# Attention scores of a two-layer encoder: three fp32r passes over high and low parts, both heads of a pair per query tile

## The chip, the cores and the metric

One core of a Trainium2 chip runs the whole program. The metric is the device time of one execution in microseconds (us). The kernel before takes 1906.68 us, the median of three runs from 1904.6 to 1908.85 us.

## What is computed

Two layers of a bidirectional encoder over 768 tokens of 1024 features: one request of 512 tokens and one of 256, with one set of weights, all in fp32. A layer has a mixer (attention with 8 heads of 64 beside a convolution over 512 channels) and a gated feed-forward part. Cut to what matters here:

```
h = rms_norm(x, norm1_g[l]) * (1 + s1) + sh1
q, k, v, cv, cg = split(h @ w_in)                      # 512 columns each
q, k = rms_norm(q per head) * q_g, rms_norm(k per head) * k_g
for (window, dilation) in ((128, 1), (512, 4), (2048, 16)):
    s = q @ k.T * ATT_SCALE + bias[distance];  masked softmax;  o = p @ v
att = the three outputs, weighted by their softmax denominators
u = silu(layer_norm(depthwise_conv(cv * sigmoid(cg), 31 taps)))
x = x + g1 * (concat([att, u]) @ w_out)
x = x + g2 * conv_ffn(rms_norm(x, norm2_g[l]) * (1 + s2) + sh2)
```

The kernel folds the three patterns into one softmax per head, with the logarithm of each distance's number of patterns added to the bias.

## The kernel before

Activations lie with features on partitions and tokens along the free dimension, in two groups: 512 tokens (g = 0) and 256 (g = 1). A projection is exact to about fp32 by three fp32r passes (`three`, lines 346 to 348): weight and activation are each split into a high part (a copy to fp32r on ACT) and a low part (the rest, a subtraction on DVE). Weights come in units of eight 128x128 blocks: `load_ahead` issues the load into a raw buffer, `consume` makes the parts `wh` (line 324, ACT) and `wl` (line 325, DVE), `release` counts a unit as used.

The order of the instructions on every engine is the order in which the program emits them. It is set by a clock in microseconds of TensorE work: `tick(dt)` advances it, `after(dt, fn)` puts a piece of work on it for later, and two background streams are dealt out by it, the attention (`side`, one step each `gap`) and the 31 taps of the convolution (`conv_bg`, by a rate). `wait(key)` emits what is due, in order and with no projection between, until the key is done.

The mixer runs in this order: gate and value columns of the convolution (`c`, `cv`, `cg`), then `v`, `q`, `k` of the first four heads; with `attention()` as background `q`, `k`, `v` of the other four; then the output projection in three parts, `pa` (attention heads 0 to 3), `pb` (heads 4 to 7) and `pc` (convolution, which also starts the next norm). A pair of heads is one 128-partition tile of `qT` and `kT`, head s on partitions 64 s to 64 s + 63.

Attention goes in steps, one per pair, group, half of 256 queries, head s and query tile qi (128 queries). `start` (line 718) emits one fp32 matmul of 64 rows, queries by all keys of the group, into a bank of PSUM. Then, each some microseconds of the clock later: `soft` (DVE adds the bias and takes the minimum, line 735; ACT takes the exponential and its sum, line 737), `normal` (reciprocal on DVE, scaling on ACT, line 746), `turn` (PE transposes `tp`, line 759; ACT evacuates to `PT`, line 760) and, when both heads have both query tiles, `values_` (`o`, line 770, the two heads on the column halves of the array; then `cah`, `cal`). At most LIVE = 5 steps are in flight. The bias of a head lies in a table `G`, loaded by `bias_table`, in three buffers.

The convolution's taps (line 554) run on DVE. After the last one, `mean` (`lm`), `centre` (`lb`, four subtractions, squares, sums), `variance` (`lv`, a power on GpSimd), `scale_shift` (`lrb`, multiply, Silu, high and low parts `cch`, `ccl`) follow for each group, and `pc` needs them.

Of the kernel before, what the change touches and what calls it, by code (L numbers as in the profile page):

```python
# [12 lines left out]
F32 = mybir.dt.float32  # L13
# [5 lines left out]
P = 128  # L19
# [18 lines left out]
RAW = 5  # L38
ACT = 28
# [5 lines left out]
GAPS = (0.9, 0.9, 0.6)  # L45
# [7 lines left out]
NORM_ACT = True  # L53


@with_exitstack
def encoder(ctx: ExitStack, tc: tile.TileContext, xT, cT, rel_bias, onehot, nlog, wada, wadaT, wada_g2, bada,
# [34 lines left out]
    # ---- emission order: a clock in microseconds of TensorE work, work due later on it, and two background streams  # L92
# [57 lines left out]
    # ---- constants  # L150
# [30 lines left out]
    # ---- the weight stream: units of 8 [P, 128] blocks, in the order of their use  # L181
# [45 lines left out]
    state = {"item": 0, "live": 0, "n": 0, "fed": 0.0, "hold": True}  # L227
# [20 lines left out]
    def ada_columns(l, kind, j, ps):  # L248
        """kind 0, 1: scale and shift of feature tile j for the half-layer; kind 2: the first gate of tiles 2j, 2j + 1."""
# [56 lines left out]
    def consume():  # L306
# [3 lines left out]
        load_ahead(i + RAW)  # L310
        r = loaded[i]
        state["fed"] = clock[0]
        if it[0] == "a":
            ada(*it[1:], r)
            return
        if it[0] == "d":
            ada_dots(*it[1:], r)
            return
# [4 lines left out]
        lo = whl.tile([P, 8 * P], F32R, tag="lo", name=f"wl{n}")  # L323
# [9 lines left out]
    def unit():  # L333
        """The next unit of the stream as two lists of blocks (hi, lo)."""
        while not ready:
            consume()
        return ready.pop(0)

    def release(n=1):
        state["live"] -= n  # L340

# [12 lines left out]
    def product(units, xs, name, keys=None):  # L354
        """Several units side by side over the contraction: [unit][group] -> psum, features on partitions."""
# [13 lines left out]
    # ---- RMSNorm with its modulation  # L369
# [14 lines left out]
    def square_sums(l, h, g, hs):  # L384
        """Returns add(j), to be called when x[j] of the group is final; after the last one the normalised tiles follow."""
# [58 lines left out]
    def part(l, gate, xs, name):  # L444
        """A part of a projection back to the residual: contraction over xs, units of 8 // len(xs) output tiles."""
# [10 lines left out]
    def last_part(l, gate, xs, name, nxt, need=None):  # L456
        """The same with one group after the other, so that the next norm runs beside it."""
# [20 lines left out]
    # ---- constants of the layers and the bias by distance  # L478
# [43 lines left out]
    # ---- mixer  # L522

    def mixer(l, K, hs, nxt):
# [112 lines left out]
        def tokens(hh, name, evacuate):  # L637
            """Columns of a half of the heads, tokens on partitions, in three pairs of token tiles."""
# [25 lines left out]
        def qk(hh, t):  # L664
# [5 lines left out]
            def evacuate(pr, ps):  # L670
# [17 lines left out]
                def turn(qn):  # L688
# [7 lines left out]
                    for i in range(2):  # L696
                        nc.scalar.activation(dst[2 * hh + i][:, pr * 256:(pr + 1) * 256], pt[:, i * 256:(i + 1) * 256],
                                             AF.Copy, scale=gain)
# [7 lines left out]
        def attention():  # L706
            steps = [(hp, g, qh, s, qi) for hp in range(4) for g, (o, w) in enumerate(GROUPS) for qh in range(w // 256)
                     for s in range(2) for qi in range(2)]
            live = [0]
            pts = {}  # L710
            for n in range(3):
                bias_table(l, n)
            base = len(tables) - 3
            last = {}
            for n, (hp, g, qh, s, qi) in enumerate(steps):
                last[2 * hp + s] = n

            def start(n):
                hp, g, qh, s, qi = steps[n]
# [11 lines left out]
                def soft():  # L731
# [6 lines left out]
                    if last[2 * hp + s] == n and 2 * hp + s + 3 < NH:  # L738
# [314 lines left out]
```

## Time and profile before

| | |
|---|---|
| median of three runs | 1906.68 us |
| span of the profiled execution | 1912.8 us |
| PE (matmul) busy | 1855.5 us, 97% |
| weight loads | 1559.1 us, 82% |
| DVE busy | 1208.8 us, 63% |
| ACT busy | 642.9 us, 34% |
| GpSimd (POOL) busy | 205.3 us, 11% |
| mean granted TensorE clock | 0.988 |
| DMA | 164.75 MB, 86 GB/s |

The profiled execution has no time of its own beside its span; the span is 6.1 us above the median of the runs. Busy times are shares of the span, and PE's contains overlapping of neighbouring matmuls, so what a piece costs on PE is read from the starts of its neighbours. The mixer of layer 0 ends at 413.7 us, where its feed-forward part begins (`u`). A clock of 1.00 is 2.4 GHz, 0.50 is 1.2 GHz.

### The profile page before, as it was taken

Reading aid. Unit: us, or ns where it says so; the run is one execution under the profiler, and the core shown is the slowest. Engines: PE = TensorE matmul, PEld = TensorE weight load, DVE = VectorE, ACT = ScalarE, POOL = GpSimd, SP = SyncE. Lnnn points to the kernel's source line nnn. Section 1 sums busy time; section 2 is a strip of 40 time slices with the busy share of each in tenths; the row PEclk is TensorE's granted clock in tenths of the full one; section 3 lists DMA queues with packets and bytes.
Section 4 is the critical chain, followed back from the end, with each engine's and each line's share of the span. In section 5 each row is a group of like instructions: output and inputs, shape, how many; then the busy total and the mean of one; then the engine's idle time right before and its main releaser. Section 6 shows DMA issues by size and latency. Waiting matters only on the chain.

```text
span 1912.8 us, 27144 instructions
## 1 busy us (share of the span) xinstructions
PE 1855.5 (97%) x11164; PEld 1559.1 (82%) x11164; DVE 1208.8 (63%) x1964; ACT 642.9 (34%) x1130; POOL 205.3 (11%) x159
## 2 busy tenths in 40 slices
PE   6999999999999999999989999999899999999999
PEld 4788676778888888888878976767788888888888
DVE  6779666776766767665578886667744343434334
ACT  3222666443313121213232256564431222222220
POOL 1002110022101000101030120000410000000010
PEclk9999999999999999999999999999999999999999
DMA  9334210113334444443111111111112122221111
GB/s 336 125 128 167 64 53 32 40 44 120 118 122 123 142 133 133 130 134 99 56 56 56 56 63 42 42 43 45 48 63 84 49 67 67 66 67 56 56 56 66
DMA packets 54267, 164.75 MB, mean 86 GB/s; under 512 B 6176, under 2 KB 15648, under 8 KB 54144
## 3 DMA queue, kind: packets, MB, share of 16 engines
q1 hardware_dynamic: 54144, 163.03, 26.9%
q8 instruction: 87, 1.43, 0.3%
q14 instruction: 36, 0.29, 0.0%
HBM read 159.83 MB, written 3.18 MB: 85 GB/s over the span
## 4 chain that ended last, share of the span: by engine, by line
PE 84%; DVE 10%; ACT 3%; issue 2%; POOL 1%; DMA 0%; SPq 0%; ACTq 0%; DVEq 0%; POOLq 0%
PE g L346 6%; PE a L346 6%; PE g L347 6%; PE a L347 6%; PE g L348 6%; PE a L348 6%; PE pd L346 5%; PE pd L347 5%; PE pd L348 5%; PE s L725 4%; DVE acc L554 2%; PE tp L759 2%; DVE wl L325 2%; PE o L770 2%; PE v L346 1%
## 5 line engine op out<-in xcount | busy, mean ns | idle before, releaser
L325 DVE TENSOR_TENSOR wl<-raw,wh 128x1024 fp32r<-128x1024 f32 x186 | 264.8, 1433 | 132.4 <-ACT wh L324 132.4
L324 ACT ACTIVATE wh<-raw 128x1024 fp32r<-128x1024 f32 x188 | 191.8, 1049 | 208.7 <-PE pd L348 208.7
L554 DVE SCALAR_TENSOR_TENSOR acc<-up,cw_sb,acc 128x783 f32<-128x783 f32 x240 | 246.6, 1028 | 3.9
L862 DVE SCALAR_TENSOR_TENSOR gc<-g,fw_sb,gc 128x511 f32<-128x511 f32 x84 | 51.4, 612 | 228.7 <-ACT gc L861 228.7
L346 PE MATMUL pd<-hh,wl 128*128 128x512 f32 (+1 forms) x576 | 193.8, 336 | 0.0
L347 PE MATMUL pd<-hl,wh 128*128 128x512 f32 (+1 forms) x576 | 193.5, 336 | 0.0
L348 PE MATMUL pd<-hh,wh 128*128 128x512 f32 (+1 forms) x576 | 192.8, 335 | 0.0
L867 POOL TENSOR_TENSOR hl<-gc,hh 128x768 fp32r<-128x768 f32 x44 | 81.8, 1859 | 900.9 <-ACT hh L866 886.0
L861 ACT ACTIVATE gc<-g,fw_sb 128x512 f32<-128x512 f32 x84 | 48.1, 573 | 382.6 <-PE g L348 382.6
L441 DVE SCALAR_TENSOR_TENSOR x<-pd,mod,x 128x512 f32<-128x512 f32 (+1 forms) x160 | 92.4, 611 | 77.8 <-PE pd L348 77.7
L292 DVE CUSTOM_DVE_ANT_0 cro<-raw,cr 128x1024 f32<-128x1024 f32 x112 | 136.7, 1221 | 2.1
L348 PEld LDWEIGHTS pd<-hh,wh 128*128 128x128 f32 x576 | 108.1, 188 | 12.5
L346 PEld LDWEIGHTS pd<-hh,wl 128*128 128x128 f32 x576 | 108.0, 188 | 12.1
L347 PEld LDWEIGHTS pd<-hl,wh 128*128 128x128 f32 x576 | 108.2, 188 | 11.5
L725 PE MATMUL s<-kT,qT 64*128 64x512 f32 (+1 forms) x192 | 95.0, 575 | 0.0
L864 ACT ACTIVATE gc<-gc 128x512 f32<-128x512 f32 x88 | 46.2, 525 | 130.1 <-DVE gc L863 130.0
L865 DVE TENSOR_TENSOR gc<-a,gc 128x512 f32<-128x512 f32 x84 | 46.8, 557 | 55.0 <-ACT gc L864 55.0
L735 DVE CUSTOM_DVE_ANT_0 sp<-s,G 128x512 f32<-128x512 f32 (+1 forms) x96 | 57.1, 596 | 23.6 <-PE s L725 23.4
L737 ACT ACTIVATE sp<-sp,nm 128x512 f32<-128x512 f32 (+1 forms) x96 | 62.1, 647 | 27.4 <-DVE nm L735 24.6
L746 ACT ACTIVATE sp<-sp,den 128x512 f32<-128x512 f32 (+1 forms) x96 | 61.8, 645 | 19.2 <-DVE den L744 19.2
L759 PEld LDWEIGHTS tp<-ident,sp 128*128 128x128 f32 x320 | 35.9, 142 | 26.0 <-ACT sp L746 8.6
L760 ACT ACTIVATE PT<-tp 128x512 f32<-128x512 f32 (+1 forms) x96 | 49.2, 517 | 22.3 <-PE tp L759 21.7
(695 smaller groups left out, 5120.9 us busy)
## 6 DMA issues: line engine op xcount, KB each, us to landing
raw<-in_w_up SPq DMA_DIRECT2D x88, 512.0 KB, 3.6
raw<-in_wadaT SPq DMA_DIRECT2D x48, 512.0 KB, 3.6
raw<-in_w_down SPq DMA_DIRECT2D x44, 512.0 KB, 4.2
raw<-in_w_in SPq DMA_DIRECT2D x40, 512.0 KB, 3.5
raw<-in_wada SPq DMA_DIRECT2D x24, 512.0 KB, 4.4
raw<-in_w_out SPq DMA_DIRECT2D x16, 512.0 KB, 4.7
G<-bt SPq DMA_DIRECT2D x16, 448.0 KB, 4.1
ad<-in_wada SPq DMA_DIRECT2D x16, 384.0 KB, 7.2
```

The lines of the kernel that those rows point to most:

```text
L292: nc.vector.tensor_tensor_reduce(out=rows["out"], in0=r, in1=rows[g], op0=ALU.mult, op1=ALU.add, scale=1.0, scalar=0.0, accum_out=mod[l][: ...
L324: nc.scalar.activation(hi, r, AF.Copy)
L325: (nc.gpsimd if n < 2 else nc.vector).tensor_tensor(lo, r, hi.bitcast(F32), op=ALU.subtract)
L346: nc.tensor.matmul(ps, wl, xh, start=first, stop=False)
L347: nc.tensor.matmul(ps, wh, xl, start=False, stop=False)
L348: nc.tensor.matmul(ps, wh, xh, start=False, stop=last)
L441: nc.vector.scalar_tensor_tensor(x[ot][:, span(g)], ps, mod[l][:, gate + ot, g:g + 1], x[ot][:, span(g)], op0=ALU.mult, op1=ALU.add)
L554: nc.vector.scalar_tensor_tensor(a, up[i][:, t:t + ACW], K["cw"][:, l, i, t:t + 1], a, op0=ALU.mult, op1=ALU.add)
L725: nc.tensor.matmul(ps[:, :w], qT[hp][64 * s:64 * s + 64, o + i * P:o + (i + 1) * P], kT[hp][64 * s:64 * s + 64, o:o + w], start=True, stop ...
L737: nc.scalar.activation(sp[:, :w], sp[:, :w], AF.Exp, scale=-1.0, bias=nm, accum_out=den)
L759: nc.tensor.transpose(pt[:, kt * P:(kt + 1) * P], sp[:, kt * P:(kt + 1) * P], ident)
L867: nc.gpsimd.tensor_tensor(lo, gc, hi.bitcast(F32), op=ALU.subtract)
```

## The change

A step of attention is now a query tile with both heads. `part_of` splits `qT` and `kT` of a pair into fp32r parts, once per pair; `start` emits six fp32r matmuls of 64 rows, the two heads in turns. The second head's softmax is due 0.6 us (AT_STEP) after the first's; a step starts when at most three heads are in flight. The gaps of the stream are longer, since a step is two heads. The low weight parts share the ring of the raw blocks, with seven buffers; a load is issued when fewer than six units are loaded and not used up. The pool of activation tiles grows from 28 to 32.

```diff
-RAW = 5
-ACT = 28
+RAW = 6
+ACT = 32
-GAPS = (0.9, 0.9, 0.6)
+GAPS = (1.2, 1.2, 0.8)
+TABLES = 3
+PTS = 3
+AT_STEP = 0.6
...
-    def load_ahead(n):
-        while len(loaded) < min(len(raws), n):
-            r = wraw.tile([P, 8 * P], F32, tag="raw", name=f"raw{len(loaded)}")
+    def load_ahead(limit=RAW):
+        while len(loaded) < len(raws) and len(loaded) - state["freed"] < limit:
+            r = wraw.tile([P, 8 * P], F32, tag="raw", name=f"raw{len(loaded)}", bufs=RAW + 1)
...
-        lo = whl.tile([P, 8 * P], F32R, tag="lo", name=f"wl{n}")
+        lo = wraw.tile([P, 8 * P], F32R, tag="raw", name=f"wl{n}", bufs=RAW + 1)
...
     def release(n=1):
         state["live"] -= n
+        state["freed"] += n
+        load_ahead()
...
-            steps = [(hp, g, qh, s, qi) for hp in range(4) ... for s in range(2) for qi in range(2)]
+            steps = [(hp, g, qh, qi) for hp in range(4) ... for qi in range(2)]
...
+            def part_of(hp, t):
+                x = (qT, kT)[t][hp]
+                hi, lo = (at(f"{'qk'[t]}{c}{l}_{hp}") for c in "hl")
+                nc.scalar.activation(hi, x, AF.Copy)
+                nc.vector.tensor_tensor(lo, x, hi.bitcast(F32), op=ALU.subtract)
+                split[hp, t] = (hi, lo)
...
-                ps = bank(f"s{tag}")
-                nc.tensor.matmul(ps[:, :w], qT[hp][64 * s:64 * s + 64, o + i * P:o + (i + 1) * P],
-                                 kT[hp][64 * s:64 * s + 64, o:o + w], start=True, stop=True)
+                banks = [bank(f"s{tag}{s}") for s in range(2)]
+                for m, (q, k) in enumerate(((q_lo, k_hi), (q_hi, k_lo), (q_hi, k_hi))):
+                    for s in range(2):
+                        nc.tensor.matmul(banks[s][:, :w], q[64 * s:64 * s + 64, o + i * P:o + (i + 1) * P],
+                                         k[64 * s:64 * s + 64, o:o + w], start=(m == 0), stop=(m == 2))
+                for s in range(2):
+                    live[0] += 1
+                    one(n, s, banks[s])
+                tick(3 * (w / 2400 + 0.003), False)
...
-                    if last[2 * hp + s] == n and 2 * hp + s + 3 < NH:
-                        bias_table(l, 2 * hp + s + 3)
+                    if last[hp] == n and 2 * hp + s + TABLES < NH:
+                        bias_table(l, 2 * hp + s + TABLES)
...
-                live[0] += 1
-                tick(0.86 * w / 512, False)
-                after(AT_DELAY[0], soft)
+                after(AT_DELAY[0] + AT_STEP * s, soft)
...
+                for t in range(2):
+                    while ("qk"[t], hp // 2) not in done:
+                        yield 1
+                    if (hp, t) not in made:
+                        made.add((hp, t))
+                        part_of(hp, t)
+                        yield 1
+                while ("v", (hp - 1) // 2 if hp else 0) not in done or live[0] + 2 > LIVE or busy[0] > 3:
+                    yield 1
```

The order of PE at the first scores of layer 0. `s` is a score bank, `q` the projection of the other heads' queries. Before:

```order
L348 MATMUL q_1966<-wh_1573,h_3h 128x256
L725 MATMUL s_1993<-kT_0_1565,qT_0_1341 128x512
L346 MATMUL q_1966<-wh_1645,h_4l 128x256
L347 MATMUL q_1966<-wl_1646,h_4h 128x256
L348 MATMUL q_1966<-wh_1645,h_4h 128x256
```

And of the change, at the second pair of layer 1 (`k` is the projection of the other heads' keys, `kh`, `kl`, `qh`, `ql` the parts, `tp` the transposes of earlier steps):

```order
L697 MATMUL hb_10632<-ident,hn_10602 128x128 x4
L351 MATMUL k_10519<-wh_10117,h_2l 128x256
...
L353 MATMUL k_10519<-wh_10154,h_4h 128x256
L741 MATMUL s_10653<-kh_1_10639,ql_1_10588 128x512
L741 MATMUL s_10654<-kh_1_10639,ql_1_10588 128x512
L741 MATMUL s_10653<-kl_1_10640,qh_1_10587 128x512
L741 MATMUL s_10654<-kl_1_10640,qh_1_10587 128x512
L741 MATMUL s_10653<-kh_1_10639,qh_1_10587 128x512
L741 MATMUL s_10654<-kh_1_10639,qh_1_10587 128x512
L786 MATMUL tp_10665<-ident,sp_10561 128x128 x2
```

Where one fp32 score stood between projections, six passes in two banks stand together; the parts of k, numbered 10639 and 10640, are emitted after the transposes `hb` numbered 10632, nine projection matmuls ahead of the scores.

The order of DVE at the end of layer 0's taps (`acc_3` is the last of the four convolution tiles, `x` the residual, `mu` the mean after the last tap). Before, in `pa`:

```order
L554 SCALAR_TENSOR_TENSOR acc_3_2602<-up_3_1114,cw_sb,acc_3_2602 128x783
L441 SCALAR_TENSOR_TENSOR x_115<-pa_5_00_3483,mod_126,x_115 128x512
L441 SCALAR_TENSOR_TENSOR x_115<-pa_5_01_3513,mod_126,x_115 128x256
L570 SCALAR_TENSOR_TENSOR mu_269<-lm_3533,mu_269 128x6
L585 TENSOR_TENSOR acc_0_690<-acc_0_690,lb_3548 128x512
```

And of the change, in `pb`:

```order
L328 TENSOR_TENSOR wl_3766<-raw_3253,wh_3765 128x1024
L559 SCALAR_TENSOR_TENSOR acc_3_2881<-up_3_1114,cw_sb,acc_3_2881 128x783 x2
L446 SCALAR_TENSOR_TENSOR x_114<-pb_4_00_3761,mod_126,x_114 128x512
L446 SCALAR_TENSOR_TENSOR x_114<-pb_4_01_3773,mod_126,x_114 128x256
L446 SCALAR_TENSOR_TENSOR x_115<-pb_5_00_3783,mod_126,x_115 128x512
L446 SCALAR_TENSOR_TENSOR x_115<-pb_5_01_3790,mod_126,x_115 128x256
L575 SCALAR_TENSOR_TENSOR mu_267<-lm_3803,mu_267 128x6
L590 TENSOR_TENSOR acc_0_690<-acc_0_690,lb_3814 128x512
```

The last tap has moved from the sixth tile of `pa` to the fifth of `pb`, eight projection tiles later, and two taps stand between the accumulations of each `pb` tile.

The order of PE from the end of `pb` to the start of `pc` in layer 0, of the change:

```order
L353 MATMUL pb_7_01_3841<-cah_3498,wh_3520 128x256
L607 MATMUL lv_3861<-ones,ls_3857 128x1 x4
L379 MATMUL lb_3870<-ident,mu_267 128x128 x2
L379 MATMUL lrb_3879<-ident,lr00r 128x128 x4
L607 MATMUL lv_3916<-ones,ls_3900 128x1 x2
L351 MATMUL pc_00_3924<-cch_3884,wl_3688 128x512
```

Before, the first `lv` stood in the fourth tile of `pb`; now nothing of the projections stands between the LayerNorm's sums and its use.

## Rows read from the trace of the kernel before

**Rows 1.** Stretches of attention, layers 0 and 1: busy us (instructions) of each engine, granted clock, DMA

```profile
189.26:353.55 164.29, 162.16 (x991) 110.49 (x988) 108.30 (x256) 104.17 (x240) 12.48 (x6) 1.00 0.16 50
1127.36:1294.73 167.37, 163.99 (x958) 112.28 (x958) 107.75 (x258) 108.51 (x246) 15.02 (x8) 0.97 0.12 37
```

**Rows 2.** Waits of PE, mixers of layers 0 and 1: us in total, times, longest

```profile
PE lv L602 <- DVE ls L589: 3.6, 2, 3.1
...
PE tp L759 <- ACT sp L746: 3.3, 4, 1.8
```

**Rows 3.** Timeline of PE round a wide score: start us, us, instruction

```profile
195.47 0.28 PE L347 MATMUL q<-wl,h_5h 128*128 128x256 f32 x1
195.58 0.28 PE L348 MATMUL q<-wh,h_5h 128*128 128x256 f32 x1
195.79 1.12 PE L725 MATMUL s<-kT,qT 64*128 64x512 f32 x2
...
197.06 0.28 PE L347 MATMUL q<-wl,h_6h 128*128 128x256 f32 x1
197.18 0.28 PE L348 MATMUL q<-wh,h_6h 128*128 128x256 f32 x1
```

**Rows 4.** Timeline of PE round a narrow score

```profile
258.93 0.28 PE L348 MATMUL k<-wh,h_1h 128*128 128x256 f32 x1
259.13 0.70 PE L725 MATMUL s<-kT,qT 64*128 64x256 f32 x2
...
259.98 0.28 PE L347 MATMUL k<-wl,h_2h 128*128 128x256 f32 x1
```

**Rows 5.** Timeline of PE, two neighbouring fp32r passes of 512 columns

```profile
354.25 0.39 PE L346 MATMUL pb<-cah,wl 128*128 128x512 f32 x1
354.48 0.39 PE L347 MATMUL pb<-cal,wh 128*128 128x512 f32 x1
```

**Rows 6.** Timeline of PE, the products with the values on two column halves

```profile
207.64 1.95 PE L770 MATMUL o<-PT,v 128*64 128x256 f32 x16
209.52 0.38 PE L346 MATMUL q<-wh,h_2l 128*128 128x256 f32 x1
```

**Rows 7.** Groups of ACT and DVE by line and form: busy us, mean ns | idle before

```profile
L737 ACT ACTIVATE sp<-sp,nm 128x512 f32<-128x512 f32 x64 | 46.0, 719 | 25.1 <-DVE nm L735 22.4 <-DVE den L744 2.6
L746 ACT ACTIVATE sp<-sp,den 128x512 f32<-128x512 f32 x64 | 45.8, 715 | 6.4 <-DVE den L744 6.4
L866 ACT ACTIVATE hh<-gc 128x768 fp32r<-128x768 f32 x44 | 37.2, 847 | 22.8 <-DVE gc L865 22.8
L737 ACT ACTIVATION_READ_ACCUMULATOR sp<-sp,nm 128x1 f32 x96 | 18.2, 190 | 0.0
...
L922 DVE TENSOR_TENSOR sq<-sq,sq 128x768 f32<-128x768 f32 x7 | 6.7, 958 | 7.1 <-ACT sq L920 6.6
```

**Rows 8.** Timeline of DVE at the end of layer 0's attention

```profile
345.16 1.01 DVE L554 SCALAR_TENSOR_TENSOR acc<-up,cw_sb,acc 128x783 f32<-128x783 f32 x1
...
355.81 1.23 DVE L325 TENSOR_TENSOR wl<-raw,wh 128x1024 fp32r<-128x1024 f32 x1 [0.60 <-ACT wh L324]
356.95 0.68 DVE L585 TENSOR_TENSOR acc<-acc,lb 128x512 f32<-128x512 f32 x1
...
358.15 1.14 DVE L441 SCALAR_TENSOR_TENSOR x<-pb,mod,x 128x512 f32<-128x512 f32 x2
```

**Rows 9.** Timeline of PE, POOL and ACT in layer 0's LayerNorm

```profile
362.19 1.05 PE L602 MATMUL lv<-ones,ls 128*128 128x1 f32 x8 [0.46 <-DVE ls L589]
...
363.58 1.01 POOL L381 TENSOR_TENSOR lr00r<-lr00v,mhalf 128x4 f32<-128x4 f32 x1 [88.64 <-DVE lr00v L379]
...
368.43 0.82 ACT L625 ACTIVATE acc<-acc,cv_sb 128x512 f32<-128x512 f32 x1 [0.59 <-DVE acc L624]
```

**Rows 10.** The stretch of ten us with the wait at `lv`, columns as in rows 1

```profile
370.00:380.00 10.00, 6.88 (x32) 5.46 (x31) 9.85 (x20) 6.14 (x10) 0.70 (x1) 0.83 0.06 23
```

**Rows 11.** DMA issues: KB each, median us to landing

```profile
raw<-in_w_in SPq DMA_DIRECT2D x40, 512.0 KB, 3.5
```

More of the change, by code (lines that the diff above doesn't have):

```diff
@@ L309, in consume @@
         state["item"] += 1
-        load_ahead(i + RAW)
+        load_ahead()
         r = loaded[i]
         state["fed"] = clock[0]
[L313 to L317, printed above, removed]
+        if it[0] != "w":
+            (ada if it[0] == "a" else ada_dots)(*it[1:], r)
+            state["freed"] += 1
+            load_ahead()
             return
@@ L696, in turn @@
                     for i in range(2):
[L697 to L698 removed]
+                        nc.scalar.activation(dst[2 * hh + i][:, pr * 256:(pr + 1) * 256],
+                                             pt[:, i * 256:(i + 1) * 256], AF.Copy, scale=gain)
                     if pr == 2:
@@ L706, in attention, with one @@
         def attention():
-            steps = [(hp, g, qh, s, qi) for hp in range(4) for g, (o, w) in enumerate(GROUPS) for qh in range(w // 256)
-                     for s in range(2) for qi in range(2)]
+            steps = [(hp, g, qh, qi) for hp in range(4) for g, (o, w) in enumerate(GROUPS) for qh in range(w // 256)
+                     for qi in range(2)]
             live = [0]
             pts = {}
-            for n in range(3):
+            split = {}
+            for n in range(TABLES):
                 bias_table(l, n)
-            base = len(tables) - 3
+            base = len(tables) - TABLES
             last = {}
-            for n, (hp, g, qh, s, qi) in enumerate(steps):
-                last[2 * hp + s] = n
-            def start(n):
-                hp, g, qh, s, qi = steps[n]
+            for n, (hp, g, qh, qi) in enumerate(steps):
+                last[hp] = n
+            def part_of(hp, t):
[4 more added lines that the diff above has]
+                split[hp, t] = (hi, lo)
+            def start(n):
+                hp, g, qh, qi = steps[n]
+                o, w = GROUPS[g]
+                i = 2 * qh + qi
+                nk = w // P
+                tag = f"{l}{hp}{g}{i}"
+                (q_hi, q_lo), (k_hi, k_lo) = split[hp, 0], split[hp, 1]
+                banks = [bank(f"s{tag}{s}") for s in range(2)]
[7 more added lines that the diff above has]
+                tick(3 * (w / 2400 + 0.003), False)
+            def one(n, s, ps):
+                hp, g, qh, qi = steps[n]
                 o, w = GROUPS[g]
@@ L754, in turn @@
                     if qi == 0:
-                        pts[hp, g, qh, s] = att.tile([P, 4, 256], F32, tag="PT", name=f"PT{tag}", bufs=3)
+                        pts[hp, g, qh, s] = att.tile([P, 4, 256], F32, tag="PT", name=f"PT{tag}", bufs=PTS)
                     PT = pts[hp, g, qh, s]
@@ L781, in values_ @@
                         done.add(("att", hp))
-                live[0] += 1
-                tick(0.86 * w / 512, False)
-                after(AT_DELAY[0], soft)
-            for n, (hp, g, qh, s, qi) in enumerate(steps):
-                while not {("q", hp // 2), ("k", hp // 2), ("v", (hp - 1) // 2 if hp else 0)} <= done or live[0] >= LIVE or busy[0] > 3:
+                after(AT_DELAY[0] + AT_STEP * s, soft)
+            made = set()
+            for n, (hp, g, qh, qi) in enumerate(steps):
+                for t in range(2):
[6 more added lines that the diff above has]
+                while ("v", (hp - 1) // 2 if hp else 0) not in done or live[0] + 2 > LIVE or busy[0] > 3:
                     yield 1
```

5 lines of the change are left out of this document (3 added, 2 removed).

## Prediction

> **What bounds the kernel now.** Read first the busy time of the engines over the two stretches from the first score matmul of a layer to the first `pb` matmul, where all attention work lies [rows 1]. TensorE (PE) is busy 162.2 of 164.3 us and 164.0 of 167.4 us; VectorE (DVE) and ScalarE (ACT) about two thirds. The order of instructions mixes attention with the projections, and PE hardly ever waits in it: the waits of PE for other engines [rows 2] show 3.3 us at the transposes (`tp`) in layer 1, and less in layer 0. So PE time taken out there is time gained, until another engine ends last. The only large PE wait of a mixer lies behind it: 3.6 us at `lv`, the sums of the convolution's LayerNorm [rows 2].
>
> Then the price of one score product, which is one fp32 matmul of 64 rows, recorded as two. In the timeline of PE three neighbours show it: from L348 before the product to L347 behind it are 1.48 us [rows 3]; without the product those two steps take 2 x 0.115 us, the pitch between the group's other rows. A 512-wide product costs 1.25 us. The same reading for 256 columns gives 1.05 - 0.23 = 0.82 us [rows 4]. The difference, 0.43 us for 256 columns, is streaming; 0.39 us of each product is fixed, the cost of entering and leaving it. An fp32r pass of 512 columns is issued every 0.23 us [rows 5], one of 256 every 0.115 us [rows 3]: less than a third of the fp32 streaming (0.86 and 0.43).
>
> **The change part by part.** *Scores.* Before: 64 wide and 32 narrow products, 64 x 1.25 + 32 x 0.82 = 106.2 us. After: 48 steps (32 wide, 16 narrow), each six passes, two heads in turns on rows 0-63 and 64-127 and in two banks. No row of before shows two row halves side by side: projections or other attention work always stand between two scores. Bounds for a wide step: three passes with no fixed part, 0.69 us, if the halves overlap wholly and entering is free; six passes and the fixed part, 0.39 + 1.38 = 1.77 us, if they do not overlap. Narrow: 0.35 and 1.10 us. The nearest row is `o`, sixteen records of eight fp32 products of 256 columns on the two column halves: 1.88 us from its start to the next matmul [rows 6], where eight at 0.43 us in a row would be 3.4. Halves of the array do overlap here, so I take three passes and one fixed part: 0.39 + 0.69 = 1.08 and 0.39 + 0.35 = 0.74 us. Sum 32 x 1.08 + 16 x 0.74 = 46.4: **-59.8 us** (ends -78.5 and -32.0). The Trainium skill ("TensorE: Matmul & The Clock Gate", Part 3, measured speedup) gives four row tiles a speedup of 3.07, not 4. An estimate from that figure, 1.54 for two tiles, would give 1.29 and 0.85 us a step and a gain of 51 us; no run here shows it.
>
> *The high and low parts.* New are 16 copies of 128x768 on ACT (0.85 us, like L866) and 16 subtractions on DVE (0.96 us, like L922) [rows 7]: 13.6 and 15.3 us beside PE. A step needs the parts of k, made last. In both layers' first pair and two more of the eight pairs, the order has only about ten projection matmuls (1.2 us) between what releases k's parts and the first score, against 0.85 + 0.96 us plus the queues in front; elsewhere several steps' work lies between. I take four times 1.5 us: **+6 us** (ends 0 and 8 x 1.8 = 14.5).
>
> *Steps of two heads.* For a pair ACT does two exponentials (0.72 + 0.19 us each), then two normalisations (0.72 us) [rows 7]. ACT's work of the stretch, 104 to 109 us [rows 1], grows by 5 us while PE's own work falls from some 160 to some 130 us; ACT comes to over 80%. Some waits must appear at the transposes: **+6 us**, 0.12 us a step (ends 0 and the rival below).
>
> *The convolution's tail.* The background taps are dealt out by the emission clock. That clock counted 0.86 us for each wide score and now 0.65 us for two, so 53 taps stood between the first softmax and `pb` in each layer and now 42 do. In layer 0 ten taps fall into the `pb` part, and the LayerNorm chain, which ran beside `pb`, now stands behind it (second and third order piece). With zero at `pb`'s start, DVE has to do an accumulate pair, a quarter-size subtraction, two weight splits, ten taps and four pairs before the last tap is done: 5 x 1.14 + 0.4 + 2 x 1.23 + 10 x 1.01 = 18.7 us [rows 8], some 17 with the overlap of neighbours; PE reaches `lm` after six and a third tiles, 13.2 us. Four us of wait. From there to the end of `pc_00`'s first tile the chain is on its own: sums, means, four subtractions and three additions at 0.68 us with two accumulate pairs between, `lv` 1.05, the power on GpSimd 1.01, the broadcast, the multiply, Silu 0.82 and a copy [rows 8, 9], then the second group's sums of the same kind, in all about 21 us, of which PE fills 11. So 14 to 15 us of waiting, plus 1.5 us of slow clock behind it: after 3 us of waiting the granted clock was 0.83 over ten us in before, between 2.4 and 1.2 GHz [rows 10]. Before lost 3.6 + 1.2 us there. Layer 0: +11.5 us. In layer 1 the last tap stands in `pb_1`; six tiles of `pb` cover most of the chain and 6.5 us stay exposed, where before had 2: +4.5 us. **+16 us** (ends 0 and 30).
>
> *Buffers and loads.* The low halves of the weights now share seven buffers with the raw blocks, so fewer loads run ahead (six units less the unreleased ones). No PE wait of before is on a load, and a block lands in 3.5 us [rows 11] while a unit feeds PE some 8 us; cost nothing. If that cover is gone, each late unit costs up to those 3.5 us. The bias tables are loaded two at once at a pair's last tiles; the order leaves over a dozen DVE instructions until their first use. Nothing.
>
> Sum: -59.8 + 6 + 6 + 16 = **-32 us**. The profiled execution spans 1912.8 us, 6 us above the median of the runs (1906.7); I carry the difference to the median: **1875 us**. About 0.2%, 4 us, is what a measurement can tell from no change.
>
> **The rivals.** *The row halves work in turns* (the change does not do what its name says): the steps cost 1.77 and 1.10 us. Then -32.0, but PE is slower against ACT, so the new waits shrink to about 6 in attention: -32 + 6 + 16 = -10 us, 1897 us. For it: no row shows row halves together. Against: `o` [rows 6].
>
> *The transposes become the wait, and it is slower than before.* Place: `tp` of the second head. On ACT its exponential and normalisation stand behind the first head's, 0.91 + 0.72 = 1.63 us later [rows 7], while the order puts only 0.6 us between the heads. If nothing else covers it, a step loses 1.03 us: 48 x 1.03 = 49 us in place of the 6: -32 + 43 = +11 us, 1918 us. It decides from 0.67 us more a step. For it: ACT over 80% busy, in order, and at most two steps in flight (four score banks, LIVE 5). Against: between a score and its transposes the order still has 5 to 9 us of PE work, a pair's softmax needs about 4, and before PE waited 3.3 us in all at the 48 transpose groups of layer 1. The Trainium skill ("TensorEngine Tiling (Array Packing)", PSUM Bottleneck) says just this, that tiling speeds up TensorE and not the evacuation of PSUM, which may then bind; by that rule the time is this rival's, and the rows of before agree only so far that ACT and DVE are two thirds busy.
>
> *The costs stay hidden*: the waits in attention do not appear and the tail costs 8 instead of 16 us, or entering a step is cheaper in fp32r: -52 to -60 us, 1850 us.
>
> **How the numbers follow.** The forecast 0.56 (1860 to 1893 by the ends of its terms), halves in turns 0.14, transposes 0.13, hidden costs 0.17. The first and last are faster, of the second somewhat over half: 0.56 + 0.17 + 0.08 = 0.81; same 0.06; slower 0.13. The range leaves out the transposes' rival and the far end of the hidden one: 1848 to 1906 us.
>
> **What would show it.** Right: score steps of about 1.1 us from neighbour to neighbour, stretches of some 138 us where 164 and 167 stood, a wait of over 10 us around `lm`, `lv` and `lrb` of layer 0 with a clock under 1.0 behind it, small waits at `tp`. Wrong: steps of 1.8 us; or PE waits at `tp` of over 0.7 us a step; or a tail whose waits are as short as before.

## The result, and the profile after

The changed kernel takes 1923.3 us (median of four runs, 1919.5 to 1927.8) against 1906.1 us before: 1.0091 of it, 95% interval 1.0070 to 1.0112. It is slower by 17 us where 32 us less were forecast. The profiled execution shown here spans 1917.7 us.

The two stretches from the first score to the first `pb` [rows 1], each followed by the one from there to the first `u` of the FFN, columns as in rows 1:

```profile
192.16:343.20 151.04, 137.31 (x1004) 106.54 (x1003) 103.00 (x250) 105.41 (x241) 11.77 (x6) 0.97 0.17 58
343.20:421.90 78.70, 64.05 (x339) 55.22 (x338) 57.89 (x93) 28.43 (x46) 5.75 (x5) 0.85 0.12 34
1135.60:1294.70 159.10, 137.85 (x966) 106.70 (x966) 102.78 (x244) 105.12 (x239) 12.97 (x6) 0.95 0.12 39
1294.70:1360.60 65.90, 58.71 (x337) 51.03 (x337) 49.42 (x85) 28.43 (x46) 5.75 (x5) 0.92 0.14 41
```

Of the kernel before, the two stretches behind `pb`:

```profile
353.55:413.70 60.15, 56.32 (x322) 48.62 (x321) 47.09 (x83) 27.66 (x44) 5.75 (x5) 0.97 0.15 44
1294.70:1349.80 55.10, 52.91 (x304) 45.52 (x303) 40.18 (x66) 23.08 (x36) 4.04 (x3) 1.00 0.17 49
```

Attention became shorter by 13.3 and 8.3 us, 21.5 together; the forecast had 47.8 (59.8 less 12). The tail became longer by 18.6 and 10.8 us, 29.4 together; the forecast had 16. PE is busy 25 us less in each attention stretch, so its work did go; but it is now idle for 14 and 21 us there, where it was idle for 2 and 3.

Two things keep these differences from being read straight off. Some work changed its stretch: `lm`, `lb`, `lrb` and `lv`, 6.7 us of PE in the attention stretches of the kernel before, stand in the tails now. Like for like, attention is shorter by about 15 us, 33 less than the forecast. And the four stretches together make 7.9 of the 17 us. The two profiled executions lie only 4.9 us apart, and the stretch from the first `u` of layer 1 to the end took 556.6 to 557.1 us in six of the eighteen profiled executions of this document and 562.9 to 565.0 in the other twelve, with no pattern by kernel. So the rest of the 17 us has no place in these traces.

The waits of PE over the whole program, largest of the mixers (total, times, longest), answer to [rows 2]:

```profile
PE tp L786 <- ACT sp L773: 20.6, 18, 4.6
...
PE lv L607 <- DVE ls L594: 14.2, 3, 5.6
...
PE lm L570 <- DVE acc L559: 5.4, 2, 4.7
```

A wide score step, to be read as [rows 3], from L353 before it to L352 behind it:

```profile
191.96 0.28 PE L353 MATMUL q<-wh,h_2h 128*128 128x256 f32 x1
192.16 0.50 PE L741 MATMUL s<-kh,ql 64*128 64x512 f32 x2
192.50 0.40 PE L741 MATMUL s<-kl,qh 64*128 64x512 f32 x2
192.74 0.40 PE L741 MATMUL s<-kh,qh 64*128 64x512 f32 x2
193.07 0.39 PE L351 MATMUL q<-wh,h_3l 128*128 128x256 f32 x1
193.29 0.28 PE L352 MATMUL q<-wl,h_3h 128*128 128x256 f32 x1
```

From L353 to L352 are 1.33 us, less the 0.23 of two projection passes: 1.10 us for both heads; a narrow step, read alike, takes 0.75. The price of the passes was foretold within 0.02 us. What failed lies round them.

**Where PE stands.** Most of its idle time lies at the changes of pairs, about 10 of the 14 us in layer 0 and 14 of the 21 in layer 1. One of them in layer 0, first ACT:

```profile
217.59 1.05 ACT L327 ACTIVATE wh<-raw 128x1024 fp32r<-128x1024 f32 x1
220.61 0.51 ACT L764 ACTIVATE sp<-sp,nm 128x256 f32<-128x256 f32 x1 [1.97 <-DVE nm L762]
...
222.15 0.51 ACT L773 ACTIVATE sp<-sp,den 128x256 f32<-128x256 f32 x1 [0.94 <-DVE den L771]
222.56 0.83 ACT L727 ACTIVATE qh<-qT 128x768 fp32r<-128x768 f32 x1
224.55 0.51 ACT L773 ACTIVATE sp<-sp,den 128x256 f32<-128x256 f32 x1 [1.16 <-DVE den L771]
224.96 0.36 ACT L255 ACTIVATE ar<-ada 128x256 f32<-128x256 f32 x1
```

then DVE:

```profile
218.67 1.23 DVE L328 TENSOR_TENSOR wl<-raw,wh 128x1024 fp32r<-128x1024 f32 x1 [2.71 <-ACT wh L327]
219.82 0.42 DVE L762 CUSTOM_DVE_ANT_0 sp<-s,G 128x256 f32<-128x256 f32 x1
...
223.42 0.96 DVE L728 TENSOR_TENSOR ql<-qT,qh 128x768 fp32r<-128x768 f32 x1 [1.37 <-ACT qh L727]
224.30 0.15 DVE L771 RECIPROCAL den<-den 128x1 f32<-128x1 f32 x1
```

and PE:

```profile
225.38 0.92 PE L261 MATMUL adb<-sel,ar 128*128 128x2 f32 x4 [4.58 <-ACT ar L255]
```

ACT stands for DVE, DVE for ACT: `wl` for `wh`, the exponential for `nm` behind `wl`, `ql` for `qh`, the next normalisation for the reciprocal behind `ql`. Each engine is two thirds busy over the stretch and does its work in order, so whatever stands in front of a queue holds a softmax behind it, and PE waits 4.58 us for a small copy at the end of that row.

Of the waits at `tp` 19.0 us lie in layer 1. The longest, at a change of pairs too, hangs on a reciprocal of 0.15 us:

```profile
1213.12 1.23 DVE L328 TENSOR_TENSOR wl<-raw,wh 128x1024 fp32r<-128x1024 f32 x1 [2.04 <-ACT wh L327]
...
1218.02 0.15 DVE L771 RECIPROCAL den<-den 128x1 f32<-128x1 f32 x1
```

```profile
1218.83 0.69 PE L786 MATMUL tp<-ident,sp 128*128 128x128 f32 x2 [4.62 <-ACT sp L773]
```

In front of it DVE's queue held two `wl`, a `ql`, a tap and two small sums, 4.9 us without a gap.

### The profile page after: what moved, and what is told of

It is laid out like the page before. It is cut to its first block, busy times and chain, and to the rows that moved or that the text cites. A ratio compares the mean times of both kernels' runs of the same rounds, so it can differ in the third digit from the quotient of the medians.

```text
span 1917.7 us, 27338 instructions
## 1 busy us (share of the span) xinstructions
PE 1814.0 (95%) x11260; PEld 1558.9 (81%) x11260; DVE 1225.2 (64%) x1980; ACT 651.7 (34%) x1146; POOL 204.3 (11%) x159
## 4 chain that ended last, share of the span: by engine, by line
PE 67%; DVE 6%; ACT 3%; issue 1%; POOL 0%; ACTq 0%; DVEq 0%; POOLq 0%
PE a L352 6%; PE g L352 6%; PE g L353 6%; PE a L353 6%; PE a L351 6%; PE g L351 6%; PE pd L352 5%; PE pd L353 5%; PE pd L351 5%; DVE wl L328 1%; PE pe L352 1%; PE pe L353 1%; PE pe L351 1%; DVE acc L559 1%; ACT wh L327 1%
## 5 line engine op out<-in xcount | busy, mean ns | idle before, releaser
L352 PE MATMUL pd<-hl,wh 128*128 128x512 f32 (+1 forms) x576 | 193.1, 335 | 0.0
L353 PE MATMUL pd<-hh,wh 128*128 128x512 f32 (+1 forms) x576 | 192.7, 334 | 0.0
L895 DVE SCALAR_TENSOR_TENSOR gc<-g,fw_sb,gc 128x511 f32<-128x511 f32 x84 | 51.4, 612 | 154.5 <-ACT gc L894 154.5
L352 PEld LDWEIGHTS pd<-hl,wh 128*128 128x128 f32 x576 | 108.2, 188 | 11.7
L353 PEld LDWEIGHTS pd<-hh,wh 128*128 128x128 f32 x576 | 108.2, 188 | 11.4
L764 ACT ACTIVATE sp<-sp,nm 128x512 f32<-128x512 f32 (+1 forms) x96 | 62.2, 648 | 52.9 <-DVE nm L762 46.6
L786 PE MATMUL tp<-ident,sp 128*128 128x128 f32 x320 | 52.0, 289 | 21.1 <-ACT sp L773 20.6
L773 ACT ACTIVATE sp<-sp,den 128x512 f32<-128x512 f32 (+1 forms) x96 | 59.9, 644 | 23.5 <-DVE den L771 23.3
L896 DVE SCALAR_TENSOR_TENSOR gc<-g,fw_sb,gc 128x511 f32<-128x511 f32 x84 | 51.8, 616 | 3.0
```

The source lines that it names most:

```text
L352: nc.tensor.matmul(ps, wh, xl, start=False, stop=False)
L353: nc.tensor.matmul(ps, wh, xh, start=False, stop=last)
L764: nc.scalar.activation(sp[:, :w], sp[:, :w], AF.Exp, scale=-1.0, bias=nm, accum_out=den)
L773: nc.scalar.activation(sp[:, :w], sp[:, :w], AF.Copy, scale=den)
L786: nc.tensor.transpose(pt[:, kt * P:(kt + 1) * P], sp[:, kt * P:(kt + 1) * P], ident)
```

## The experiments

Each run was measured beside the kernel before on the same chip, so kernels are compared by their ratios to it; runs of one kernel spread by about 1%. The table has the median, the ratio to before with its interval, and by PE's timeline the lengths of attention (first score to `pb`) and tail (`pb` to `u`) in layers 0 and 1.

| kernel | us | ratio [95%] | attention | tail |
|---|---|---|---|---|
| before | 1906.1 | 1 | 164.3, 167.4 | 60.2, 55.1 |
| changed | 1923.3 | 1.0091 [1.0070, 1.0112] | 151.0, 159.1 | 78.7, 65.9 |
| e1 clock as before | 1899.5 | 0.9954 [0.9926, 0.9982] | 161.1, 155.6 | 61.1, 54.7 |
| e2 taps as before | 1915.1 | 1.0040 [1.0017, 1.0064] | 165.6, 168.5 | 63.6, 54.3 |
| e3 pairs in fp32 | 1909.4 | 1.0008 [0.9986, 1.0031] | 144.5, 149.9 | 79.5, 66.2 |
| e4 buffers alone | 1913.9 | 1.0031 [1.0000, 1.0062] | 174.6, 164.8 | 60.9, 54.9 |
| e5 fp32 pairs, clock | 1892.7 | 0.9916 [0.9884, 0.9947] | 155.7, 152.8 | 61.3, 54.6 |
| e6 no splits | 1901.0 | 0.9966 [0.9941, 0.9991] | 142.9, 149.5 | 79.1, 66.6 |
| e7 parts ahead | 1891.9 | 0.9933 [0.9904, 0.9963] | 158.8, 154.9 | 59.8, 55.5 |
| e8 heads apart | 1924.3 | 1.0092 [1.0063, 1.0122] | 153.5, 160.9 | 79.3, 67.7 |
| e9 longer spacing | 1896.2 | 0.9943 [0.9922, 0.9964] | 156.5, 156.9 | 59.6, 59.6 |
| e10 shorter spacing | 1911.9 | 1.0032 [1.0013, 1.0051] | 156.7, 162.5 | 60.8, 60.5 |
| e11 cal later | 1876.8 | 0.9846 [0.9818, 0.9874] | 148.8, 145.0 | 59.0, 58.0 |
| e12 and wl on GpSimd | 1870.8 | 0.9790 [0.9763, 0.9817] | 142.2, 140.5 | 59.0, 57.9 |
| e13 three passes, all edits | 1879.5 | 0.9847 [0.9819, 0.9875] | 151.9, 150.0 | 59.4, 54.6 |
| e14 before, cal later | 1908.8 | 1.0012 [0.9986, 1.0039] | 163.6, 160.6 | 60.0, 59.6 |
| e15 changed, cal later | 1915.1 | 1.0061 [1.0037, 1.0084] | 151.3, 154.8 | 78.9, 68.2 |
| e16 e12, old buffers | 1860.7 | 0.9771 [0.9739, 0.9802] | 142.2, 141.8 | 58.8, 58.0 |

### The order's clock and the taps: e1, e2

```diff
 e1:  in start
-                tick(3 * (w / 2400 + 0.003), False)
+                tick(2 * 0.86 * w / 512, False)
 e2:  in start, behind that tick
+                conv_bg["acc"] += (2 * 0.86 * w / 512 - 3 * (w / 2400 + 0.003)) * conv_bg["rate"]
+                conv_step()
```

> The clock of the order counts 1.72 and 0.86 us for a score step, as before, instead of 0.65 and 0.33; nothing else differs from the changed kernel. Theory W (the scores got cheaper as forecast; attention waits because too little TensorE work lies between a score and its transposes, and the tail because ten taps were dealt out too late): the taps go back to their places, so the tail from pb to u returns from 79 and 66 us to about 62 and 57, but delays counted on this clock now hold less projection work, so the waits at tp grow, from 21 to 30 us or more; sum about 1923 - 26 + 10 = 1907 us. Rival S (the splits at the start of each pair cost the time, spacing does not matter): the tail comes back and nothing else moves, 1897 us. Rival T (the emission clock is the whole cause): waits at tp and tail both return to those of before, 1880 us or less.

> Only the background taps are dealt out as if a step still counted 1.72 and 0.86 us; the clock of everything else is as in the changed kernel. Theory W: the tail from pb to u returns to about 62 and 57 us (-26 us), the attention stretches stay at 151 and 159 us or grow by up to 5 us each because VectorE has ten more taps in them; 1897 to 1907 us. A theory in which the tail's waits come from the new ring of buffers or the loads: the tail stays at 75 us or more, 1920 us.

In both the tail is back, so the displaced taps made it. But giving the taps back alone moves most of the time into attention (e2):

```profile
190.80:356.40 165.60, 143.89 (x1021) 109.69 (x1020) 116.96 (x268) 107.65 (x245) 12.55 (x6) 0.95 0.16 52
1132.30:1300.80 168.50, 141.83 (x993) 110.71 (x994) 111.53 (x262) 109.34 (x249) 12.77 (x7) 0.93 0.11 36
```

In e2 attention grows by 14.6 and 9.4 us where I expected at most 5. PE's busy time, with the LayerNorm's sums back in the stretch, is 10.6 us of that; 13.4 us are more waiting, though DVE is under 72% busy. e1 gains more than e2, and my expectation for its waits was wrong in sign: those at `tp` are 14.8 us in the two stretches and did not grow to 30. Its time, 1899.5 us, is near rival S, but not as S has it: attention did move, by +10.0 and -3.5 us.

### What the passes and the splits are worth: e3, e6, e8

```diff
 e3:  in start, and part_of is not called
-                for m, (q, k) in enumerate(((q_lo, k_hi), (q_hi, k_lo), (q_hi, k_hi))):
-                    for s in range(2):
...
+                for s in range(2):
+                    nc.tensor.matmul(banks[s][:, :w], qT[hp][64 * s:64 * s + 64, o + i * P:o + (i + 1) * P],
+                                     kT[hp][64 * s:64 * s + 64, o:o + w], start=True, stop=True)
 e6:  qT and kT written as fp32r at once, and part_of is not called
-                for m, (q, k) in enumerate(((q_lo, k_hi), (q_hi, k_lo), (q_hi, k_hi))):
+                for m, (q, k) in enumerate(((qT[hp], kT[hp]),) * 3):
 e8:  in start
-                for m, (q, k) in enumerate(((q_lo, k_hi), (q_hi, k_lo), (q_hi, k_hi))):
-                    for s in range(2):
+                for s in range(2):
+                    for m, (q, k) in enumerate(((q_lo, k_hi), (q_hi, k_lo), (q_hi, k_hi))):
```

> The order of the changed kernel with its clock, pairs of heads and buffers, but each head's score is one fp32 product as before, and no high and low parts are made. Theory W: TensorE takes 60 us more in attention, of which about 25 fills its present waits: the stretches come to 165 to 170 us, the tail stays at 79 and 66 us, about 1935 us (12 above the changed kernel). Rival S (splits are what holds attention): the waits at pair changes vanish with them, and the stretches show 151 + 30 - 10 = 170 us or more only from TensorE's work with tp waits under 5 us in all, 1940 to 1945 us. If the three passes had brought nothing at all the time would stay at 1923 us.

> The changed kernel with its six passes but without splits: q and k are rounded once, on their way from PSUM, and the same tile serves as high and low part; the low parts and so two of the three products of the score are left out as values, not as passes. Order and clock as in the changed kernel. Theory S: attention 143 and 148 us instead of 151 and 159, the tail 79 and 66 as there, about 1904 us. Theory W (only the spacing counts, splits are beside TensorE): 1918 to 1923 us.

> The changed kernel with the three passes of one head before the three of the other, instead of the heads in turns. If the halves overlap only for neighbouring passes on different rows: just one of five transitions overlaps, a wide step takes about 1.55 to 1.77 us instead of 1.10 and a narrow one 0.95 to 1.10 instead of 0.75, TensorE has 20 to 25 us more a kernel, part of it in present waits: 1930 to 1940 us. If TensorE runs ahead over several passes of one half: 1.10 us and 1923 us.

No theory had e3 right: with slower scores it is faster than the changed kernel. Its PE timeline shows why, in a wide step of two heads:

```profile
194.56 0.28 PE L353 MATMUL q<-wh,h_5h 128*128 128x256 f32 x1
194.76 1.13 PE L739 MATMUL s<-kT,qT 64*128 64x512 f32 x4
195.82 0.39 PE L351 MATMUL q<-wh,h_6l 128*128 128x256 f32 x1
196.04 0.28 PE L352 MATMUL q<-wl,h_6h 128*128 128x256 f32 x1
```

1.48 us from neighbour to neighbour, as much as one head alone took before [rows 3]; a narrow step 1.06, against 1.05 for one head [rows 4]. Two fp32 products on the two row halves cost what one cost. Putting the heads side by side is worth 106.2 - (32 x 1.25 + 16 x 0.83) = 52.9 us; the three passes add 32 x 0.15 + 16 x 0.08 = 6.1 us to that, and nothing else. For these 6 us the kernel makes 16 copies and 16 subtractions. e6 has the passes without them (it leaves out the low parts, so its scores are rounded), and its attention (waits at `tp` 1.3 and 13.5 us) is

```profile
190.50:333.40 142.90, 135.89 (x1005) 105.44 (x1004) 96.83 (x243) 100.68 (x235) 11.78 (x6) 0.98 0.20 63
1125.00:1274.50 149.50, 134.99 (x966) 105.15 (x965) 97.12 (x238) 100.40 (x233) 12.69 (x6) 0.97 0.13 41
```

8.1 and 9.6 us shorter than in the changed kernel: the splits cost 17.7 us there, not 6, and in the time 0.9966 against 1.0091, intervals apart. The longest waits at `tp` in layer 1 are 3.8 and 3.4 us where the changed kernel has 4.6 and 3.4, so the splits make little of those. e8 tells that the order of the six passes doesn't matter: wide steps of 1.32 to 1.34 us from neighbour to neighbour, and the time of the changed kernel.

### The buffers: e4, e16

e4 is the kernel before with the shared ring of seven buffers, the loads by what was freed and 32 tiles of activations; e16 is e12 (below) with those of the kernel before.

> The kernel before with only the change of the buffers: seven buffers shared by raw blocks and low halves, loads by what was freed, 32 tiles of activations. My prediction and theory W: no difference, within 4 us of the kernel before. Rival (the ring costs): a few us slower in the projections and the FFN, 1910 to 1925 us, with waits of PE or of ACT for the loads.

> The fastest kernel so far (fp32 pairs, clock of before, cal later, weights' low halves on GpSimd; 1870.8 us, 0.979 of before), with the buffers and loads of the kernel before: five raw tiles, low halves in a ring of their own, 28 tiles of activations. Its trace has five waits of ACT's copy wh for a load of w_up, 25 us in all, where the kernel before has none. If the new ring costs what the run of the buffers alone hints at (1.0031 of before, 1.0000 to 1.0062): the waits go and 1864 to 1868 us. If those waits are covered: 1870 us as it was.

The new ring makes four waits of ACT's `wh` for loads of `w_up`, 19.4 us in all in e4 and 19.5 in the changed kernel, that the kernel before doesn't have. In e16 they are gone. What they cost stays open: e4, 0.3% slower, lies between its two theories and its interval just touches no change; the intervals of e16 and e12 overlap.

### What holds attention when the scores are cheap: e5, e7, e9, e10

e5 is e3 with the tick of e1. e7 is e1 with the parts of the second and fourth pair made before the narrow steps of the pair ahead. e9 and e10 are e5 with other delays:

```diff
 e9:
-AT_DELAY = (0.5, 2.5, 2.2, 2.0)
+AT_DELAY = (0.5, 3.5, 3.2, 2.0)
 e10:
+AT_DELAY = (0.5, 1.8, 1.5, 2.0)
```

> The pairs of heads in fp32 (no high and low parts), with the clock of before for the order, so that the taps stand where they stood. Theory S, formed on the first runs (putting the two heads on the two row halves is the gain, 1.25 us for both where one took 1.25; three fp32r passes add only 0.15 us to that, and the splits they need cost 16 us in ACT's and DVE's chains): the tail returns to 61 and 55 us, attention grows by 5 to 8 us a layer for the ten taps, about 1893 us. If taps cost in attention what they save in the tail, as in the run with the taps alone: 1905 us.

> Three passes with the clock of before, and in two of the four pairs of a layer the parts are made two steps earlier, before the narrow steps of the pair ahead. Against the run with the clock alone (1899 us; waits at the first scores for the parts 6 us in layer 0 and 11.5 in layer 1). If the splits cost by their latency at the pair's start: the waits at s halve, 1890 us. If they cost by the time they take on ACT and DVE: the waits move to tp and the time stays at 1897 to 1902 us.

> The pairs in fp32 with the clock of before (1892.7 us, waits at tp 9.3 and 8.1 us), and one microsecond more on the order's clock between softmax and normalisation and between normalisation and transposes (2.5 and 2.2 become 3.5 and 3.2). If the waits at tp are the latency of the chain against the work laid between: the waits fall to 3 us a layer or less and the clock dips behind them go, about 1880 us. If they come from the queues of ACT and DVE (everything behind moves with it): the waits stay or move to s and hb, 1890 to 1897 us.

> The same kernel with the two spacings shortened by 0.7 us (1.8 and 1.5). Latency: 0.7 to 1.4 us less cover at each of 48 pairs of transposes, waits at tp grow by 15 to 30 us, 1905 to 1920 us. Queues: waits as they are, 1890 to 1897 us.

e5 came out as foretold in time and tail; its attention grew by 11.2 and 2.9 us against e3, not by 5 to 8 each. e7's time is that of its latency case, and the waits at `s` for parts fall from 17.5 to 2.7 us. But the waits at `tp`, `o` and `hb` grow from 16.1 to 28.9, as in its other case, attention is only 3.0 us shorter than in e1, and the intervals of e1 and e7 overlap. What e7's edit is worth is not shown. The spacing is near its best already: in e10 PE waits twice as long at `tp` (17.9 and 19.8 us against 9.3 and 8.1),

```profile
PE tp L784 <- ACT sp L771: 17.9, 16, 5.8
```

while in e9 `tp` falls to 7.7 and 2.1 us and `hb` and `o` take 8.7 instead in layer 1. So both theories hold half: too little cover makes a wait, more cover only moves it along the queues. In e5's DVE, by line in layer 0's attention (busy, mean ns | idle before it), the stops can be seen:

```profile
L328 DVE TENSOR_TENSOR wl<-raw,wh 128x1024 fp32r<-128x1024 f32 x6 | 7.3, 1224 | 8.1 <-ACT wh L327 8.1
...
L804 DVE TENSOR_TENSOR cal<-o,cah 128x256 fp32r<-128x256 f32 x12 | 5.1, 424 | 19.6 <-ACT cah L803 19.6
```

Before each `cal` DVE stands 1.6 us for the copy `cah`, issued right ahead of it, with taps that wait for nothing queued behind. In the kernel before the same stop is there, with PE busy 162.2 of 164.3 us beside it:

```profile
L779 DVE TENSOR_TENSOR cal<-o,cah 128x256 fp32r<-128x256 f32 x12 | 5.1, 422 | 18.0 <-ACT cah L778 18.0
```

### The stops taken away: e11 to e15

```diff
 e11 (on e5), e14 (on the kernel before), e15 (on the changed kernel):  in values_
-                    nc.vector.tensor_tensor(lo[:, sl], po[:, :256], hi[:, sl].bitcast(F32), op=ALU.subtract)
-                    if g == 1:
-                        done.add(("att", hp))
+                    def low():
+                        nc.vector.tensor_tensor(lo[:, sl], po[:, :256], hi[:, sl].bitcast(F32), op=ALU.subtract)
+                        if g == 1:
+                            done.add(("att", hp))
+                    after(1.2, low)
 e12 (on e11), e13 (e7 with both):  in consume
-        (nc.gpsimd if n < 2 else nc.vector).tensor_tensor(lo, r, hi.bitcast(F32), op=ALU.subtract)
+        (nc.gpsimd if n < 2 or side["gen"] is not None else nc.vector).tensor_tensor(lo, r, hi.bitcast(F32), op=ALU.subtract)
```

> The pairs in fp32 with the clock of before (1892.7 us); the subtraction cal, which makes the low part of the attention's output, is issued 1.2 us of the order's clock behind the copy cah that it waits for, instead of right behind it. In that kernel DVE stands 19.6 us for cah in layer 0's attention, with taps and softmaxes queued behind. If these stops in DVE's queue are what holds the softmax chains: they go, tp waits fall by half, 1884 to 1888 us. If DVE has slack enough there: 1892 us as before.

> The same, and while attention runs the low halves of the weights are made by GpSimd instead of DVE: 16 of them a kernel, 1.22 us each on DVE and some 2.4 us on GpSimd, so DVE also loses its 8 us of standing for the copies wh in layer 0. If DVE's queue is what holds attention: another 4 to 8 us, 1878 to 1884 us. If GpSimd slows DVE, or the weights now come late to the projections: waits of PE on wl, 1890 us or more.

> Three passes with the clock of before, parts ahead in two of four pairs (1891.9 us), and both of these edits. Theory S: passes and fp32 pairs stay within 5 us of each other, the 6 us of TensorE that the passes save against the splits' time: 1876 to 1886 us. If the passes' gain was only covered by DVE's stops, it is now seen: 1870 to 1875 us, below the fp32 pairs.

> The kernel before with one edit alone: cal 1.2 us later than cah. There PE is busy all through attention, so that DVE's stops have nothing to give: 1903 to 1908 us, no difference, if the stops matter only once the scores are cheap. If they cost the kernel before as well (through the tail and the next stage): 1892 to 1900 us.

> The changed kernel with the same edit alone; its clock and its taps stay, so the tail stays at 79 and 66 us. If DVE's stops for cah hold its attention as they held that of the fp32 pairs (15 us there): 1908 us. If the stops at the pair changes, for the parts and the weights, outweigh them: 1915 to 1922 us.

In e11 the stop is gone and not a busy microsecond with it; the same lines:

```profile
L328 DVE TENSOR_TENSOR wl<-raw,wh 128x1024 fp32r<-128x1024 f32 x6 | 7.3, 1224 | 12.7 <-ACT wh L327 12.7
...
L806 DVE TENSOR_TENSOR cal<-o,cah 128x256 fp32r<-128x256 f32 x12 | 5.0, 418 | 0.2
```

Attention falls by 6.9 and 7.8 us and `tp` waits from 17.4 to 10.5. Of these 14.7 us PE's waiting is 6.0; the other 8.5 are a shorter busy time, at a granted clock of 0.98 and 0.99 where e5 had 0.97 and 0.96. e12 takes `wl` off DVE and attention comes to

```profile
190.90:333.10 142.20, 136.57 (x972) 102.72 (x972) 108.78 (x250) 101.24 (x239) 27.21 (x12) 1.00 0.20 65
1106.10:1246.60 140.50, 134.12 (x945) 102.22 (x945) 107.76 (x251) 102.92 (x243) 29.31 (x14) 0.99 0.15 47
```

with DVE as busy as in e11, 108.8 us in layer 0. So on the fp32 pairs the account closes: their scores are 52.9 us cheaper, e5's attention is 23.3 us shorter than that of the kernel before, e12's 49.0. The kernel before, which PE holds, gains nothing from the later `cal` (e14); `wl` on GpSimd was not tried on it. The changed kernel with the later `cal` (e15) takes 1915.1 us, on the edge of its second case, and its interval overlaps that of the changed kernel. In the profile its tail stays, of attention layer 1 alone gets shorter, by 4.3 us, and a wait of 4.0 us at `tp` is left. On three passes both edits are clear of noise: e13 has 0.9847 where e7 has 0.9933, with attention 6.9 and 4.9 us shorter. With every edit the three passes stay behind the fp32 pairs, 0.9847 against 0.9790 (e13, e12): the 6 us of passes don't pay for the splits. e12 and e16 are the fastest versions, faster than both kernels.

## Why the prediction was wrong

- **Scores, -59.8 us: right in sum.** Measured 32 x 1.10 + 16 x 0.75 = 47.2 us, so -59.0. The rival of halves in turns falls (1.10, not 1.77). The estimate of 1.29 and 0.85 us, worked out from a figure of the Trainium skill ("TensorE: Matmul & The Clock Gate", Part 3), was too dear: in e3 two tiles overlap without visible loss (1.48 us for two products and for one). What the prediction missed is that 52.9 of it are the pairing's and not the passes'.
- **High and low parts, +6: the term was too small by 12.** e6 shows 17.7 us. I priced the chain at the pair's start alone; the copies and subtractions also stand before softmaxes in both queues, as the row at 222 us shows.
- **Steps of two heads, +6: the step that failed.** "PE time taken out there is time gained, until another engine ends last", and that engine I sought by busy shares. No engine became full: ACT, forecast at over 80%, was busy 70% and 66% of the stretches, DVE 68% and 65%, and they stop for each other in order. PE's waiting in attention rose by 29.5 us where both terms had 12. Attention missed the forecast by 26 us as the stretches stand, by 33 like for like; the splits are 12 of that. The stops of DVE behind `cah` and `wh`, there before and covered by PE's work, are the place of what is left, as far as the fp32 pairs show it: taking them away brought 14.7 us (e11) and another 11.1 (e12). On three passes both together brought 11.8 (e13 against e7). On the changed kernel itself only `cal` was tried, with no gain clear of noise; how its 21 us divide among `wh`, the granted clock (0.97 and 0.95, before 1.00 and 0.97) and the rest stays open.
- **The transposes' rival named the place, but not the mechanism.** Waits at `tp` rose from 4.6 to 20.6 us, 0.33 us a step where it needed 0.67, and 14 of them lie at the three changes of pairs in layer 1, not step by step. That its 1918 us lie near the measured time is luck. The Trainium skill ("TensorEngine Tiling (Array Packing)", PSUM Bottleneck) warned of evacuation as a possible next bound. Here `tp` waits for the normalisation (`sp`), not for the evacuation behind it, and what binds isn't the rate of ACT's and DVE's work but its place in the queues: in e11 and e12 both engines are as busy as in e5 (DVE 108.8 us in layer 0, in e5 107.8), and attention is 14.7 and 25.8 us shorter.
- **The tail, +16: mechanism right, 13 us too small.** The waits of layer 0, `lm` 4.7, `lv` 8.5 and `lrb` 1.1 us, are the 14 to 15 foretold; those of layer 1, about 7 us, the 6.5. The displaced taps were ten in layer 0 as foretold, but three in layer 1 (44 before and 41 now between first score and `pb`). What was missing is in PE's busy time, which grew by 7.7 and 5.8 us, and of that I had 1.5 in one layer. About half is the work that moved here from attention, 6.7 us at the speed it had there and 9.2 here. The rest goes with the granted clock behind the waits: 0.85 and 0.92 over the two tails where before had 0.97 and 1.00; `pb` and `pc`, as many products as before, are busy 4.4 us longer. The stretches to compare with [rows 10], most of the first and the last at 1.2 GHz:

```profile
360.00:370.00 10.00, 8.60 (x36) 7.78 (x36) 6.20 (x12) 1.26 (x2) 0.00 (x0) 0.56 0.18 52
370.00:380.00 10.00, 2.83 (x18) 1.99 (x16) 6.86 (x14) 4.72 (x8) 1.01 (x1) 0.78 0.00 0
380.00:390.00 10.00, 7.49 (x22) 6.10 (x23) 7.29 (x15) 7.10 (x13) 0.70 (x1) 0.53 0.00 1
```

- **Buffers, 0:** not contradicted, not settled. Of the 49 us between forecast and result the two attention stretches and the two tails hold 39.7; e4's 0.3% is the one run that hints at a place for the rest.

## What to carry to other kernels

Busy shares do not tell what a faster engine will gain: where two engines hand work to each other in order, list for each the time that it stands and for whom, and take those stops away first; they may cost nothing until the engine that covered them gets faster (`cal`: nothing in e14, 14.7 us of attention in e11). Try the two halves of a change apart: here the pairing was nearly the whole gain, and the passes cost more than they brought. Where a clock of the emission deals out background work, a cheaper foreground piece silently moves that work later; before comparing two stretches, count whether the same work stands in them.

## What was not expected of the hardware

Two fp32 products of 64 rows on the two row halves took 1.48 us from neighbour to neighbour, the same as one; six fp32r passes took 1.33 in either order of heads.

Once the granted clock fell after a short wait. In e4 PE, busy from 170 to 185 us at a clock of 1.00, waits 0.27 us for DVE and then 1.02 us for a load,

```profile
189.57 0.64 PE L245 MATMUL ada<-raw,sc 128*32 128x256 f32 x8 [1.02 <-DMA raw<-in_wada]
```

and then, busy throughout, is granted 1.2 instead of 2.4 GHz for most of twenty us (granted clock 0.54 and 0.61):

```profile
190.00:200.00 10.00, 10.00 (x28) 5.28 (x24) 4.22 (x10) 4.01 (x7) 2.29 (x1) 0.54 0.05 19
200.00:210.00 10.00, 10.00 (x41) 7.51 (x40) 4.17 (x10) 4.64 (x10) 0.00 (x0) 0.61 0.01 2
```

Twenty us at a mean of 0.575 are 8.5 us of PE lost, most of the 10.3 by which e4's attention of layer 0 is longer than that of the kernel before [rows 1]. In e13 PE waits 1.02 us at `tp` at 200 us and is granted 1.00 from 190 to 220 us, so a wait of that length doesn't always do this; why it did in e4 stays open. A comparison of single stretches of two runs can be off by that much.

GpSimd's `wl` holds up DVE's taps: in e12 the fifty taps of layer 0's attention take

```profile
L559 DVE SCALAR_TENSOR_TENSOR acc<-up,cw_sb,acc 128x783 f32<-128x783 f32 x50 | 56.9, 1139 | 0.4
```

1139 ns each against 1026 in e5, 5.6 us more, beside six `wl` of 2.45 us on GpSimd. All of it falls on four taps that began while a `wl` ran; one of them, and its `wl`:

```profile
229.82 3.15 DVE L559 SCALAR_TENSOR_TENSOR acc<-up,cw_sb,acc 128x783 f32<-128x783 f32 x1
```

```profile
229.76 2.38 POOL L328 TENSOR_TENSOR wl<-raw,wh 128x1024 fp32r<-128x1024 f32 x1 [3.58 <-ACT wh L327]
```

The four took 1.66 to 3.15 us and each ended 0.83 us behind the end of its `wl`, however early it had begun; the other 46 took 1.03 us. The Trainium skill ("SBUF — State Buffer", Terms) says that the two engines share a port pair which one holds for a whole instruction; these taps agree. DVE's busy time in attention did not fall by the move (108.8 us in layer 0 in e11 and e12, 106.1 and 107.8 in layer 1). So moving `wl` paid by the stops that it took away, not by the work.
